# A gated delta rule on one core: from a pipeline of single steps to rounds of two steps

## The chip, the cores and the metric

One core of a Trainium2 chip runs the whole program. The metric is the device time of one execution in microseconds, as the median of several runs. Engines are called as in the profile: PE is TensorE's matmul, PEld its weight load, DVE is VectorE, ACT is ScalarE, POOL is GpSimd, SP is SyncE, which here only issues DMAs.

## The reference, cut to what matters

A backbone of two layers over 512 latent tokens and 256 context tokens of width 1024, in float32. Layer 0 is a bidirectional gated delta rule, layer 1 is attention. The change lies in layer 0's recurrence over chunks of 64 tokens, run for 16 value heads in both directions. Head size is 128 for keys and values. The state s is 128 x 128 per head and direction.

```python
def step(s, xs):
    qk_i, qd_i, kd_i, u_i, w_i, gl_i = xs
    v_new = u_i - jnp.einsum('bhcd,bhde->bhce', w_i, s)
    o = jnp.einsum('bhcd,bhde->bhce', qd_i, s) + jnp.einsum('bhcs,bhse->bhce', qk_i, v_new)
    s = s * gl_i[..., None, None] + jnp.einsum('bhcd,bhce->bhde', kd_i, v_new)
    return s, o
```

u and w are the inverse of a triangular matrix T, made per chunk beforehand, times scaled values and keys. The kernel uses T r with r = v - (decay) k s in place of u - w s, which is the same v_new, and applies the decays as scale factors of single tokens.

## The kernel before, in words

**Tiles.** Both directions run at once: one half of the 128 partitions holds a chunk of the forward pass, the other half a chunk of the backward pass. There are 12 chunk steps s (4 over the context, 8 over the latents). Each is cut into four parts p of four value heads (two key heads). So the loop has 48 steps x = 4 s + p. Each token tile (two chunks of 64) is met twice, since each direction reaches it from its own end; `visit` says which time it is.

**One step x.** `products(x)` (line 1490) makes, for each of the two key heads j, a PSUM tile `ks` with four products of 128x64 shape: k s and q s for both directions (line 1508). DVE turns the k s half into `r` (line 1511), ACT scales the q s half into the output tile `O` or, at the second visit, into `o` (line 1514), and POOL decays the state `S` (line 1517). At the second visit POOL also adds `o` to `O` (line 1520). `solve(x)` (line 1523) makes T r with 64x64 tiles in `pr` (line 1534), ACT copies it to `vn` (line 1536) and makes four decayed copies `vd` (line 1546; by DVE, line 1544, for s = 0). `update(x)` (line 1549) makes Q K v_new in `pq` (line 1560) and the state update in `su` (line 1568), both with 64x64 tiles. DVE then adds `pq` to `O` (line 1574) and `su` to the state (line 1582, two instructions; a copy, line 1580, for s = 0). Step 11 updates no state. Each of the matmuls that the code names runs as two instructions.

**Order.** The loop at line 1687 issues products(x), solve(x - 1), update(x - 2), so three steps are in flight. Inside `manual_schedule` (line 1678) PE, DVE, ACT and POOL take the instructions in the order of the program; the loads on SP aren't in that order and go out as their buffers come free. `load_step` (line 1462) asks for a chunk step's k, q, v, T, QK and the turned keys kt. All but q have one buffer for even and one for odd steps.

**PSUM.** The pool `psC` holds two buffers of `ks`, one of `pr`, one of `pq` and one of `su`. `pr` and `pq` are allocated with room for four heads' pairs, of which half is written. A buffer is given to a new tile when everything that read the old one is done.

**Around it.** Between the steps the loop issues `square_o` (ACT, sums of squares of finished outputs), a chain of small steps on DVE and POOL for the norm's factors, and the beginning of the output projection: `out_load`, `gate_load` (DMA), `out_high` (ACT, the weights' upper half), `out_low` (POOL, the lower half), `out_scale` (ACT), `out_turn` (PE, transposes into a `ks` buffer), `out_gated`, `out_rest` (DVE), `out_product` (PE, in the buffers of `pr`, `pq`, `su`).

Of the kernel before, what the change touches and what calls it, by code (L numbers as in the profile page):

```python
# [75 lines left out]
def raw(ap, offset, dims):  # L76
    return bass.AP(ap.tensor, ap.offset + offset, [list(ap.ap[0])] + [list(d) for d in dims])


def bcast(ap, axis, n):  # L80
    a = ap.unsqueeze(axis)
    shape = list(a.shape)
    shape[axis] = n
    return a.to_broadcast(shape)


def backbone(tc, a, out):
# [1335 lines left out]
    def square_o(t, h):  # L1423
        S.activation(ojk[:, h % 2], O[t][:, h], AF.Square, accum_out=oss[:, SLOT[t], h:h + 1])
# [21 lines left out]
    if True:  # L1446
# [38 lines left out]

        live = {}

        def products(x):  # L1490

            s, p = divmod(x, 4)
            if p == 0:
                load_step(s)
            t, visit = where(s)
            kq, kt, v, Tt, QK = loads[s]
            if s == 0:
                live[x] = [v[:, 4 * p:4 * p + 4]]
                return
            r = ch.tile([P, 4, P], F32, tag="r", name=f"r{x}", bufs=2)  # L1500
            o = O[t][:, 4 * p:4 * p + 4] if visit == 0 else ch.tile([P, 4, P], F32, tag="o", name=f"o{x}", bufs=2)
            for j in range(2):
                hh = 2 * p + j
                ks = pcx.tile([P, 2, 2, P], F32, tag="ks", name=f"ks{x}_{j}", bufs=2)
                for w in range(2):
                    for d in range(2):
                        r0 = (visit ^ d) * 64
                        T.matmul(ks[r0:r0 + 64, w], kq[w][:, hh, r0:r0 + 64], St[hh][:, d], start=True, stop=True)  # L1508
                for i in range(2):
                    h = 2 * hh + i  # L1510
                    V.scalar_tensor_tensor(r[:, 2 * j + i], ks[:, 0, i], negV[:, visit, t, h:h + 1], v[:, h], ALU.mult, ALU.add)
                for i in range(2):
                    h = 2 * hh + i
                    S.activation(o[:, 2 * j + i], ks[:, 1, i], AF.Copy, scale=egV[:, visit, t, h:h + 1])
                if s < 11:
                    g_ = glb[:, visit, :, t, 2 * hh:2 * hh + 2]
                    G.tensor_tensor(St[hh], St[hh], bcast(g_, 3, P), ALU.mult)  # L1517
            if visit == 1:
                oh = O[t][:, 4 * p:4 * p + 4]
                G.tensor_tensor(oh, oh, o, ALU.add)  # L1520
            live[x] = [r]

        def solve(x):

            s, p = divmod(x, 4)
            t, visit = where(s)
            Tt = loads[s][3]
            r, = live[x]
            pr_ = pcx.tile([P, 2, 4, P], F32, tag="pr", name=f"pr{x}", bufs=1)
            for i in range(2):  # L1530
                for j in range(2):
                    for hf in range(2):
                        r0, o0 = hf * 64, (hf ^ j) * 64
                        T.matmul(pr_[o0:o0 + 64, j, i], Tt[r0:r0 + 64, 4 * p + 2 * j + i, :], r[r0:r0 + 64, 2 * j + i], start=True, stop=True)
            vn = ch.tile([P, 4, P], F32, tag="vn", name=f"vn{x}", bufs=2)
            S.copy(vn.rearrange("p (j i) d -> p j i d", j=2), pr_[:, :, 0:2])
            vd = None
            if s < 11:
                vd = ch.tile([P, 4, P], F32, tag="vd", name=f"vd{x}", bufs=2)
                for c in range(4):  # L1540
                    h = 4 * p + c
                    el = (elX if c > 1 else elV)[:, visit, t, h:h + 1]
                    if s == 0:
                        V.tensor_scalar(vd[:, c], vn[:, c], el, None, ALU.mult)
                    else:
                        S.activation(vd[:, c], vn[:, c], AF.Copy, scale=el)
            live[x] = [vn, vd]

        def update(x):

            s, p = divmod(x, 4)
            t, visit = where(s)
            kq, kt, v, Tt, QK = loads[s]
            vn, vd = live.pop(x)
            po = pcx.tile([P, 2, 4, P], F32, tag="pq", name=f"pq{x}", bufs=1)
            for i in range(2):
                for j in range(2):
                    for hf in range(2):
                        r0, i0 = hf * 64, (hf ^ j) * 64
                        T.matmul(po[r0:r0 + 64, j, i], QK[i0:i0 + 64, 4 * p + 2 * j + i, :], vn[i0:i0 + 64, 2 * j + i], start=True, stop=True)  # L1560
            if s < 11:
                su = pcx.tile([P, 2, 2, 2, P], F32, tag="su", name=f"su{x}", bufs=1)
                for j in range(2):
                    hh = 2 * p + j
                    for c0 in (0, 64):
                        for d in range(2):
                            r0 = (visit ^ d ^ j) * 64
                            T.matmul(su[c0:c0 + 64, d ^ j, j], kt[r0:r0 + 64, hh, c0:c0 + 64], vd[r0:r0 + 64, 2 * j:2 * j + 2], start=True, stop=True)  # L1568
            oh = O[t][:, 4 * p:4 * p + 4]
            ov = oh.rearrange("p (j i) d -> p j i d", j=2)  # L1570
            if s == 0:
                S.copy(ov, po[:, :, 0:2])
            else:
                V.tensor_tensor(ov, po[:, :, 0:2], ov, ALU.add)
            if s < 11:
                for j in range(2):
                    hh = 2 * p + j
                    sj = raw(su[:, 0, 0] if j == 0 else su[:, 1, 1], 0, [[512 - 1024 * j, 2], [P, 2], [1, P]])
                    if s == 0:
                        V.tensor_copy(St[hh], sj)  # L1580
                    else:
                        V.tensor_tensor(St[hh], sj, St[hh], ALU.add)  # L1582

    PASS = ((0, 0), (0, 1), (1, 0))
    SCALE = 128.0 ** -0.5
# [93 lines left out]
    def some(steps, n):  # L1681
        for f_ in steps[:n]:
            f_()
        del steps[:n]

    squares = [(t, h) for t in (1, 0, 5) for h in range(VH)]
    for x in range(50):
        if x == 47:
            out_scale(0)
        if x < 48:  # L1690
            products(x)
        if 0 <= x - 1 < 48:
# [775 lines left out]
```

## Time and profile before

| what | us |
|---|---|
| median of 3 runs | 1166.88 |
| lowest and highest run | 1165.75, 1167.48 |
| span of the profiled execution (the profile gives no other time of it) | 1170.6 |
| PE busy | 1131.2 (97%) |
| PEld busy | 925.0 (79%) |
| DVE busy | 801.6 (68%) |
| ACT busy | 730.6 (62%) |
| POOL busy | 568.8 (49%) |
| first and last state product (line 1508) start | 560.7 and 728.8 |

Times in the profile count from the start of the span. A row of the timeline gives start, duration, engine, line, operation, what it writes and reads, and how many alike were merged; in brackets stands how long the engine was idle before it and what released it. A row of the busy times gives a stretch, its length, each engine's busy time with the number of instructions, the clock granted to PE (1.00 is full), the share of the DMA engines' time and GB/s. A matmul's end is modelled, and the next one is issued before it.

### The profile page before, as it was taken

The page shows a single profiled execution, that of the slowest core. Times are in us where ns is not written, and L with a number is a line of the kernel's source. Part 1 is how long each engine was busy: PE and PEld are TensorE (multiplying, and loading weights), DVE is VectorE, ACT ScalarE, POOL GpSimd, SP SyncE. Part 2 cuts the span into 40 slices and gives each one's busy share as a digit, 9 for nine tenths or more (in the row PEclk, how much of TensorE's full clock was granted, in tenths as well). Part 3 has the DMA queues.
Part 4 walks back from the last instruction along what each step waited for, and adds up shares of the span by engine and source line. Part 5 has one row for each costly group of instructions (what it writes and reads, how often), then busy time and mean ns, then how long its engine had stood idle before and what let it go on. Part 6 is the DMA issues. An engine that isn't in the chain of part 4 may idle for free. (4 is left out here: it accounts for less than half of the span.)

```text
span 1170.6 us, 27671 instructions
## 1 busy us (share of the span) xinstructions
PE 1131.2 (97%) x10767; PEld 925.0 (79%) x10767; DVE 801.6 (68%) x1657; ACT 730.6 (62%) x1908; POOL 568.8 (49%) x471
## 2 busy tenths in 40 slices
PE   5999999999999999989999999999999999999996
PEld 3677888888888888878666666788887889999885
DVE  5595565688897889673778888345557476667646
ACT  5434444477877889654678998775753246666731
POOL 0154000149989999910475587655745143130810
PEclk9999999999999999989999999999999999999998
DMA  9677754675748767445999994575844112101313
GB/s 366 240 272 223 279 154 140 210 184 174 215 124 258 246 219 261 162 160 190 243 260 246 276 257 113 198 214 183 247 135 135 36 55 73 37 19 55 109 72 90
DMA packets 118901, 208.73 MB, mean 178 GB/s; under 512 B 12497, under 2 KB 77170, under 8 KB 114930
## 3 DMA queue, kind: packets, MB, share of 16 engines
q1 hardware_dynamic: 98834, 195.32, 54.1%
q10 hardware_dynamic: 19936, 11.64, 3.4%
q8 instruction: 85, 1.39, 0.5%
q14 instruction: 46, 0.38, 0.1%
HBM read 166.16 MB, written 40.67 MB: 177 GB/s over the span
## 5 line engine op out<-in xcount | busy, mean ns | idle before, releaser
L1517 POOL TENSOR_TENSOR S<-S,glb 128x512 f32<-128x512 f32 x80 | 81.8, 1044 | 103.9 <-PE ks L1508 103.9
L1675 PE MATMUL po<-woh,y 128*128 128x512 f32 x384 | 130.0, 403 | 0.7 <-ACT y L1651 0.7
L1624 POOL TENSOR_TENSOR wol<-wo,woh 128x1024 fp32r<-128x1024 f32 x32 | 77.2, 2414 | 55.7 <-ACT woh L1617 51.9
L791 POOL TENSOR_TENSOR X<-X,tmp 128x62 f32<-128x62 f32 (+15 forms) x93 | 99.7, 1072 | 7.3
L790 POOL TENSOR_TENSOR tmp<-L,X 128x62 f32<-128x62 f32 (+15 forms) x93 | 92.8, 998 | 6.8
L904 PE MATMUL g_v<-uh,wh_v 128*128 128x512 f32 (+1 forms) x256 | 88.6, 346 | 2.7 <-DVE sil_v L938 2.7
L904 PE MATMUL g_z<-uh,wh_z 128*128 128x512 f32 (+1 forms) x256 | 89.0, 348 | 0.0
L919 DVE SCALAR_TENSOR_TENSOR acc_v<-g_v,cwv,acc_v 128x510 f32<-128x510 f32 (+3 forms) x128 | 78.3, 614 | 13.8 <-ACT acc_v L911 10.2
L904 PE MATMUL g_v<-uh,wl_v 128*128 128x512 f32 (+1 forms) x256 | 86.9, 339 | 0.0
L904 PE MATMUL g_v<-ul,wh_v 128*128 128x512 f32 (+1 forms) x256 | 86.8, 339 | 0.0
L904 PE MATMUL g_z<-uh,wl_z 128*128 128x512 f32 (+1 forms) x256 | 86.8, 339 | 0.0
L904 PE MATMUL g_z<-ul,wh_z 128*128 128x512 f32 (+1 forms) x256 | 86.7, 339 | 0.0
L1675 PEld LDWEIGHTS po<-woh,y 128*128 128x128 f32 x384 | 72.7, 189 | 16.0 <-ACT y L1651 0.9
L1675 PE MATMUL po<-wol,y 128*128 128x512 f32 x192 | 76.0, 396 | 0.9 <-POOL wol L1624 0.9
L1649 DVE SCALAR_TENSOR_TENSOR pt<-pt,og,z 128x128 f32<-128x128 f32 x96 | 34.4, 358 | 34.1 <-PE pt L1640 31.8
L1582 DVE TENSOR_TENSOR S<-su,S 128x512 f32<-128x512 f32 x80 | 51.6, 686 | 6.1 <-PE su L1568 3.9
L904 PEld LDWEIGHTS g_v<-uh,wh_v 128*128 128x128 f32 x256 | 49.0, 191 | 8.3 <-DVE sil_v L938 2.9
L464 POOL TENSOR_TENSOR wl_k<-w_k,wh_k 128x1024 fp32r<-128x1024 f32 x8 | 19.1, 2393 | 74.3 <-ACT wh_k L460 74.3
L1508 PE MATMUL ks<-S,ck 128*64 128x256 f32 x352 | 55.2, 392 | 0.0
L492 DVE SCALAR_TENSOR_TENSOR acc_k<-g_k,cwv,acc_k 128x510 f32<-128x510 f32 (+3 forms) x64 | 39.2, 615 | 23.3 <-ACT acc_k L485 21.6
L893 POOL TENSOR_TENSOR wl_z<-w_z,wh_z 128x1024 fp32r<-128x1024 f32 x3 | 7.3, 2445 | 97.6 <-ACT wh_z L890 97.6
L904 PEld LDWEIGHTS g_z<-uh,wh_z 128*128 128x128 f32 x256 | 48.9, 191 | 5.6 <-DVE sil_v L938 0.2
(448 smaller groups left out, 3384.8 us busy)
## 6 DMA issues: line engine op xcount, KB each, us to landing
aw<-in_ada_late SPq DMA_DIRECT2D x16, 1024.0 KB, 7.6
wo<-in_dn_w_out SPq DMA_DIRECT2D x32, 512.0 KB, 3.7
cv<-v_d SPq DMA_DIRECT2D x48, 256.0 KB, 8.0
aw<-in_ada_first SPq DMA_DIRECT2D x8, 1024.0 KB, 11.9
w_z<-in_dn_w_in SPq DMA_DIRECT2D x16, 512.0 KB, 4.8
w_v<-in_dn_w_in SPq DMA_DIRECT2D x16, 512.0 KB, 4.5
v_d<-vt ACTq DMA_DIRECT2D x16, 384.0 KB, 4.6
cT<-t_d SPq DMA_DIRECT2D x12, 512.0 KB, 8.1
```

Source lines behind the costliest of these rows:

```text
L464: E.tensor_tensor(khl[h][1][:, :, :m], kw.pop(h)[:, :, :m], khl[h][0][:, :, :m], ALU.subtract)
L492: V.scalar_tensor_tensor(acc[:, c0 + lo:c0 + hi], ps[:, lo + j - 2:hi + j - 2], cwv[:, j, 8 + h:9 + h], acc[:, c0 + lo:c0 + hi], ALU.mult, ...
L790: G.tensor_tensor(tv, bcast(L[:, :, j + 1:, j], 3, j + 1), bcast(X[:, :, j, 0:j + 1], 2, n), ALU.mult)
L791: G.tensor_tensor(X[:, :, j + 1:, 0:j + 1], X[:, :, j + 1:, 0:j + 1], tv, ALU.subtract)
L904: T.matmul(ps[:, :m], w[:, k], u[:, k, c0:c0 + m], start=k == 0 and n_ == 0, stop=k == KT - 1 and n_ == 2)
L919: V.scalar_tensor_tensor(acc[:, c0 + lo:c0 + hi], ps[:, lo + j - 2:hi + j - 2], cwv[:, j, ct:ct + 1], acc[:, c0 + lo:c0 + hi], ALU.mult, A ...
L1508: T.matmul(ks[r0:r0 + 64, w], kq[w][:, hh, r0:r0 + 64], St[hh][:, d], start=True, stop=True)
L1517: G.tensor_tensor(St[hh], St[hh], bcast(g_, 3, P), ALU.mult)
L1582: V.tensor_tensor(St[hh], sj, St[hh], ALU.add)
L1624: G.tensor_tensor(wl, raws.pop(n), halves[n][0], ALU.subtract)
L1649: V.scalar_tensor_tensor(pj, pj, og, raw(z, off, [[st_, 2], [1, 64]]), ALU.mult, ALU.mult)
L1675: T.matmul(acc[:, nh], y[i][:, j, :], ww[k][:, nh * 512:(nh + 1) * 512], start=h == 0 and x == 0, stop=h == VH - 1 and x == 2)
```

## The change

The single steps become 23 rounds of two steps x and y = x + 1, and a tail for steps 46 and 47 written out by hand. In a round PE gets the state products of both steps first (four `ks` tiles, still two buffers), then the 64x64 products: the state update of the round before's first step, Q K v_new of both steps of the round before, T r of x, the state update of the round before's second step, T r of y. The `pr` tile holds T r of both steps, and `pq` Q K v_new of both. Their copies to `vn` come at the end of the round, the decayed copies `vd` among the next round's state products, and the additions of `pq` to `O` one round later still, among the state products. Squares, the norm's chain and the output projection's first pieces are distributed anew. In the cut diff "..." marks what is left out; `states(x, j)` has the body of the old loop over j, and `solve`, `intra`, `update` have the old matmuls.

```diff
--- before
+++ after
-        def products(x):
...
-            for j in range(2):
-                hh = 2 * p + j
-                ks = pcx.tile([P, 2, 2, P], F32, tag="ks", name=f"ks{x}_{j}", bufs=2)
-                for w in range(2):
-                    for d in range(2):
-                        r0 = (visit ^ d) * 64
-                        T.matmul(ks[r0:r0 + 64, w], kq[w][:, hh, r0:r0 + 64], St[hh][:, d], start=True, stop=True)
-                for i in range(2):
-                    h = 2 * hh + i
-                    V.scalar_tensor_tensor(r[:, 2 * j + i], ks[:, 0, i], negV[:, visit, t, h:h + 1], v[:, h], ALU.mult, ALU.add)
-                for i in range(2):
-                    h = 2 * hh + i
-                    S.activation(o[:, 2 * j + i], ks[:, 1, i], AF.Copy, scale=egV[:, visit, t, h:h + 1])
-                if s < 11:
-                    g_ = glb[:, visit, :, t, 2 * hh:2 * hh + 2]
-                    G.tensor_tensor(St[hh], St[hh], bcast(g_, 3, P), ALU.mult)
-            if visit == 1:
-                oh = O[t][:, 4 * p:4 * p + 4]
-                G.tensor_tensor(oh, oh, o, ALU.add)
             live[x] = [r]
...
+        def begin(x):
...
+            live["o", x] = o
+
+        def states(x, j):
...
+            hh = 2 * p + j
+            ks = pcx.tile([P, 2, 2, P], F32, tag="ks", name=f"ks{x}_{j}", bufs=2)
...
+        def joined(x):
...
+            if s and visit == 1:
+                oh = O[t][:, 4 * p:4 * p + 4]
+                G.tensor_tensor(oh, oh, live["o", x], ALU.add)
+
+        def paired(x, tag):
+
+            if x % 2 == 0:
+                shared[tag] = pcx.tile([P, 2, 4, P], F32, tag=tag, name=f"{tag}{x}", bufs=1)
+            i0 = x % 2 * 2
+            return shared[tag][:, :, i0:i0 + 2]
...
-            pr_ = pcx.tile([P, 2, 4, P], F32, tag="pr", name=f"pr{x}", bufs=1)
+            pr_ = paired(x, "pr")
...
-            S.copy(vn.rearrange("p (j i) d -> p j i d", j=2), pr_[:, :, 0:2])
...
+            live[x] = [vn, pr_]
+
+        def kept_new(x):
+
+            vn, pr_ = live[x]
+            S.copy(vn.rearrange("p (j i) d -> p j i d", j=2), pr_)
+            vd = ch.tile([P, 4, P], F32, tag="vd", name=f"vd{x}", bufs=2) if x < 44 else None
+        def decayed_new(x, cs):
...
+            vn, vd = live[x]
+            for c in cs:
+                h = 4 * p + c
+                el = (elX if c > 1 else elV)[:, visit, t, h:h + 1]
+                if s == 0:
+                    V.tensor_scalar(vd[:, c], vn[:, c], el, None, ALU.mult)
+                else:
+                    S.activation(vd[:, c], vn[:, c], AF.Copy, scale=el)
-        def update(x):
...
-            po = pcx.tile([P, 2, 4, P], F32, tag="pq", name=f"pq{x}", bufs=1)
+        def intra(x):
...
+            po = paired(x, "pq")
...
+        def added(x):
...
+            ov = O[t][:, 4 * p:4 * p + 4].rearrange("p (j i) d -> p j i d", j=2)
             if s == 0:
-                S.copy(ov, po[:, :, 0:2])
+                S.copy(ov, po)
             else:
-                V.tensor_tensor(ov, po[:, :, 0:2], ov, ALU.add)
+                V.tensor_tensor(ov, po, ov, ALU.add)
+        def update(x):
...
@@ -1684,40 +1725,84 @@
-    for x in range(50):
-        if x == 47:
-            out_scale(0)
-        if x < 48:
-            products(x)
-        if 0 <= x - 1 < 48:
-            solve(x - 1)
-        if x == 48:
-            pt = out_gated(0)
-        if x == 49:
-            out_product(0, 2)
-        if 0 <= x - 2 < 48:
-            update(x - 2)
-        if 18 <= x < 34 or x >= 35:
-            for t, h in squares[:2]:
-                square_o(t, h)
-            del squares[:2]
-        if x == 1:
+
+    def squared(n):
+        for t, h in squares[:n]:
+            square_o(t, h)
+        del squares[:n]
+
+    for rd in range(23):
+        x, y = 2 * rd, 2 * rd + 1
+        first, second = x - 2, x - 1
+        begin(x)
+        begin(y)
+        decayed_new(first, (0,))
+        states(x, 0)
+        decayed_new(first, (1,))
+        if x >= 4:
+            added(x - 4)
+        states(x, 1)
+        decayed_new(first, (2, 3))
+        joined(x)
+        states(y, 0)
+        decayed_new(second, (0,))
+        if x >= 4:
+            added(x - 3)
+        states(y, 1)
+        decayed_new(second, (1, 2, 3))
+        joined(y)
+        if rd:
+            update(first)
+            intra(first)
+            intra(second)
+        solve(x)
+        if rd:
+            update(second)
+        solve(y)
+        squared(4 if 9 <= rd < 17 or rd == 18 else 6 if rd in (19, 20) else 0)
+        if rd == 22:
+            out_high(0)
+            out_low(0)
+        kept_new(x)
+        kept_new(y)
+        if rd == 0:
             V.tensor_tensor(or2, rq, rq, ALU.mult)
-        if x in (43, 44, 45, 46):
-            some(chain, (4, 6, 6, 99)[x - 43])
+        if rd in (20, 21, 22):
+            some(chain, (0, 10, 99)[rd - 20])
         if x in (28, 32, 36, 40):
             with tc.issue_after(mark[0]):
                 (out_load if x < 36 else gate_load)((x - 28) // 4 % 2)
-        if x in (45, 46):
-            out_high(x - 45)
-        if x in (47, 48):
-            out_low(x - 47)
-        if x == 47:
-            out_load(2)
-            out_turn(0)
-        if x == 48:
-            out_rest(0, pt)
-            out_scale(1)
+    begin(46)
+    begin(47)
+    out_high(1)
+    out_low(1)
+    states(46, 0)
+    added(42)
+    out_scale(0)
+    states(46, 1)
+    added(43)
+    joined(46)
+    states(47, 0)
+    states(47, 1)
+    joined(47)
+    intra(44)
+    intra(45)
+    out_turn(0)
+    solve(46)
+    kept_new(46)
+    solve(47)
+    kept_new(47)
+    added(44)
+    added(45)
+    out_load(2)
+    pt = out_gated(0)
+    out_rest(0, pt)
+    intra(46)
+    out_scale(1)
+    intra(47)
+    out_product(0, 2)
+    added(46)
+    added(47)
     out_turn(1)
```

More of the change, by code (lines that the diff above doesn't have):

```diff
@@ L1484, in load_step @@
             loads[s] = (kq, kt, v, Tt, QK)
-        live = {}
-        def products(x):
+        live, shared = {}, {}
+        def begin(x):
             s, p = divmod(x, 4)
@@ L1495, in products @@
             t, visit = where(s)
-            kq, kt, v, Tt, QK = loads[s]
+            v = loads[s][2]
             if s == 0:
@@ L1518, in products @@
-            if visit == 1:
-                oh = O[t][:, 4 * p:4 * p + 4]
-                G.tensor_tensor(oh, oh, o, ALU.add)
-            live[x] = [r]
+            live[x] = [r]
+            live["o", x] = o
+        def states(x, j):
+            s, p = divmod(x, 4)
+            if s == 0:
+                return
+            t, visit = where(s)
+            kq, _, v, _, _ = loads[s]
+            (r,), o = live[x], live["o", x]
+            hh = 2 * p + j
+            ks = pcx.tile([P, 2, 2, P], F32, tag="ks", name=f"ks{x}_{j}", bufs=2)
+            for w in range(2):
+                for d in range(2):
+                    r0 = (visit ^ d) * 64
+                    T.matmul(ks[r0:r0 + 64, w], kq[w][:, hh, r0:r0 + 64], St[hh][:, d], start=True, stop=True)
+            for i in range(2):
+                h = 2 * hh + i
+                V.scalar_tensor_tensor(r[:, 2 * j + i], ks[:, 0, i], negV[:, visit, t, h:h + 1], v[:, h], ALU.mult, ALU.add)
+            for i in range(2):
+                h = 2 * hh + i
+                S.activation(o[:, 2 * j + i], ks[:, 1, i], AF.Copy, scale=egV[:, visit, t, h:h + 1])
+            if s < 11:
+                g_ = glb[:, visit, :, t, 2 * hh:2 * hh + 2]
+                G.tensor_tensor(St[hh], St[hh], bcast(g_, 3, P), ALU.mult)
@@ L1523, in solve @@
+        def joined(x):
+            s, p = divmod(x, 4)
+            t, visit = where(s)
+            if s and visit == 1:
+                oh = O[t][:, 4 * p:4 * p + 4]
+                G.tensor_tensor(oh, oh, live["o", x], ALU.add)
[4 more added lines that the diff above has]
+            return shared[tag][:, :, i0:i0 + 2]
         def solve(x):
             s, p = divmod(x, 4)
-            t, visit = where(s)
@@ L1535, in solve @@
             vn = ch.tile([P, 4, P], F32, tag="vn", name=f"vn{x}", bufs=2)
[L1536 to L1546, printed above, removed]
+            live[x] = [vn, pr_]
[3 more added lines that the diff above has]
+            vd = ch.tile([P, 4, P], F32, tag="vd", name=f"vd{x}", bufs=2) if x < 44 else None
             live[x] = [vn, vd]
-        def update(x):
+        def decayed_new(x, cs):
+            if not 0 <= x < 44:
+                return
             s, p = divmod(x, 4)
             t, visit = where(s)
-            kq, kt, v, Tt, QK = loads[s]
-            vn, vd = live.pop(x)
-            po = pcx.tile([P, 2, 4, P], F32, tag="pq", name=f"pq{x}", bufs=1)
+            vn, vd = live[x]
+            for c in cs:
+                h = 4 * p + c
+                el = (elX if c > 1 else elV)[:, visit, t, h:h + 1]
+                if s == 0:
+                    V.tensor_scalar(vd[:, c], vn[:, c], el, None, ALU.mult)
+                else:
+                    S.activation(vd[:, c], vn[:, c], AF.Copy, scale=el)
+        def intra(x):
+            s, p = divmod(x, 4)
+            QK = loads[s][4]
+            vn, _ = live[x]
+            po = paired(x, "pq")
             for i in range(2):
@@ L1560, in update @@
                         T.matmul(po[r0:r0 + 64, j, i], QK[i0:i0 + 64, 4 * p + 2 * j + i, :], vn[i0:i0 + 64, 2 * j + i], start=True, stop=True)
[L1561 to L1568, printed above, removed]
@@ L1569, in update @@
-            oh = O[t][:, 4 * p:4 * p + 4]
-            ov = oh.rearrange("p (j i) d -> p j i d", j=2)
+            live["po", x] = po
+        def added(x):
+            s, p = divmod(x, 4)
+            t, _ = where(s)
+            po = live.pop(("po", x))
+            ov = O[t][:, 4 * p:4 * p + 4].rearrange("p (j i) d -> p j i d", j=2)
             if s == 0:
-                S.copy(ov, po[:, :, 0:2])
+                S.copy(ov, po)
             else:
-                V.tensor_tensor(ov, po[:, :, 0:2], ov, ALU.add)
@@ L1575, in update @@
[L1575 to L1582, printed above, removed]
+                V.tensor_tensor(ov, po, ov, ALU.add)
+        def update(x):
+            s, p = divmod(x, 4)
+            if s == 11:
+                return
+            t, visit = where(s)
+            kt = loads[s][1]
+            _, vd = live[x]
+            su = pcx.tile([P, 2, 2, 2, P], F32, tag="su", name=f"su{x}", bufs=1)
+            for j in range(2):
+                hh = 2 * p + j
+                for c0 in (0, 64):
+                    for d in range(2):
+                        r0 = (visit ^ d ^ j) * 64
+                        T.matmul(su[c0:c0 + 64, d ^ j, j], kt[r0:r0 + 64, hh, c0:c0 + 64], vd[r0:r0 + 64, 2 * j:2 * j + 2], start=True, stop=True)
+            for j in range(2):
+                hh = 2 * p + j
+                sj = raw(su[:, 0, 0] if j == 0 else su[:, 1, 1], 0, [[512 - 1024 * j, 2], [P, 2], [1, P]])
+                if s == 0:
+                    V.tensor_copy(St[hh], sj)
+                else:
+                    V.tensor_tensor(St[hh], sj, St[hh], ALU.add)
```

## The prediction

> **What bounds the kernel now.** I read the page first, then the busy time by stretch, then the timeline of one step, then the waits at both ends of the stage.
>
> ```profile
> span 1170.6 us, 27671 instructions
> ```
> ```profile
> core 0: us, PE busy (x) PEld busy (x) DVE busy (x) ACT busy (x) POOL busy (x), PEclk, DMA share, GB/s
> 560.70:624.00 63.30, 60.55 (x980) 39.66 (x976) 47.24 (x110) 45.13 (x137) 41.37 (x39) 1.00 1.06 251
> 624.00:724.30 100.30, 100.30 (x1718) 65.00 (x1714) 82.36 (x191) 92.41 (x332) 69.26 (x70) 1.00 0.91 241
> 724.30:738.50 14.20, 11.75 (x160) 7.70 (x157) 8.16 (x21) 8.07 (x22) 9.65 (x11) 0.88 0.23 57
> ```
> ```profile
> 640.00:660.00 20.00, 20.00 (x352) 12.94 (x344) 15.97 (x37) 18.82 (x69) 10.91 (x11) 1.00 1.03 279
> ...
> 680.00:700.00 20.00, 20.00 (x338) 12.83 (x338) 16.66 (x39) 18.28 (x68) 17.58 (x16) 1.00 0.98 263
> ...
> 730.00:735.00 5.00, 2.55 (x45) 1.58 (x38) 3.06 (x7) 3.38 (x11) 3.87 (x3) 0.97 0.15 43
> 735.00:740.00 5.00, 5.00 (x31) 3.53 (x32) 1.51 (x4) 1.05 (x1) 2.54 (x2) 0.69 0.72 197
> ```
>
> The delta rule's steps with a state product run from 560.70 to 738.5. From 624 on PE is never idle, so one step costs what PE takes for it. ACT (94% from 640 to 660) and DVE (80%) have little to spare.
>
> One step, by the timeline (start, duration, engine, line):
>
> ```profile
> 640.25 1.04 PE L1568 MATMUL su<-vd,ckt 64*64 64x256 f32 x16
> ...
> 641.23 0.65 PE L1508 MATMUL ks<-S,ck 128*64 128x256 f32 x4
> 641.29 0.69 ACT L1546 ACTIVATE vd<-vn,elV 128x128 f32<-128x128 f32 x2
> 641.45 1.29 DVE L1582 TENSOR_TENSOR S<-su,S 128x512 f32<-128x512 f32 x2 [0.19 <-PE su L1568]
> ...
> 641.71 0.60 PE L1508 MATMUL ks<-S,cq 128*64 128x256 f32 x4
> 641.89 0.68 ACT L1546 ACTIVATE vd<-vn,elX 128x128 f32<-128x128 f32 x2
> ...
> 642.14 0.60 PE L1508 MATMUL ks<-S,ck 128*64 128x256 f32 x4
> ...
> 642.40 2.05 POOL L1517 TENSOR_TENSOR S<-S,glb 128x512 f32<-128x512 f32 x2 [1.73 <-PE ks L1508]
> ...
> 642.57 0.60 PE L1508 MATMUL ks<-S,cq 128*64 128x256 f32 x4
> 642.66 1.17 DVE L1511 SCALAR_TENSOR_TENSOR r<-ks,negV,cv 128x128 f32<-128x128 f32 x4
> ...
> 643.11 0.67 PE L1534 MATMUL pr<-r,cT 64*64 64x128 f32 x16
> 643.36 1.20 ACT L1514 ACTIVATE O<-ks,egV 128x128 f32<-128x128 f32 x4 [0.20 <-DVE r L1511]
> ...
> 643.59 0.62 PE L1560 MATMUL pq<-vn,cQK 64*64 64x128 f32 x16
> ...
> 644.03 1.04 PE L1568 MATMUL su<-vd,ckt 64*64 64x256 f32 x16
> 644.35 0.69 DVE L1574 TENSOR_TENSOR O<-pq,O 128x512 f32<-128x512 f32 x1 [0.51 <-PE pq L1560]
> 644.44 0.59 ACT L1536 COPY vn<-pr 128x512 f32<-128x512 f32 x1
> ...
> 645.00 0.65 PE L1508 MATMUL ks<-S,ck 128*64 128x256 f32 x4
> ```
>
> The reader should see the period, 645.00 - 641.23 = 3.77 us, and its parts: four groups of state products (ks) 0.43 apart (the first 0.48), T r (pr) 0.48, Q K v (pq) 0.44, state updates (su) 0.97. The last ks group would let the next begin at 643.00; pr begins at 643.11. su needs 4 x 0.216 = 0.86 and takes 0.97. So each change between the 128x64 and the 64x64 shape costs 0.11 of PE, and the first group after it 0.05 more: 0.16 each, 0.32 a step.
>
> **The change part by part.** The edits that only regroup PE leave its matmuls as they are: two steps had four changes of shape and have two. Saved: 2 x 0.16 = 0.32 us a round. PE's own work in a round: 2 x 3.77 - 0.32 = 7.22. Rounds with state products before the tail: steps 4 to 45, so 21. Alone this is 21 x 0.32 = 6.7 us of gain.
>
> *The ks buffers.* Four ks tiles are now written one after another, and there are still two buffers; before, 1.9 us of 64x64 work stood between every two tiles and the next two. A buffer's trip, from its first matmul, by the rows: its second group starts at 0.48 and lasts 0.60, done at 1.08. The first reader follows by 0.09 (POOL at 642.40 after 642.31). Two r on DVE: four took 1.17 at 0.34 each, so 0.28 apart, together 0.62. ACT's scaling of the same tile starts only behind both (642.66 + 0.62 = 643.28, ACT 643.36 with "<-DVE r"): 0.08. Two scalings, likewise: 0.64. Then PE again, which needs the price of a released wait:
>
> ```profile
> 558.24 1.29 DVE L1580 COPY S<-su 128x512 f32<-128x512 f32 x2
> ...
> 559.68 1.09 PE L1568 MATMUL su<-vd,ckt 64*64 64x256 f32 x16 [0.74 <-DVE S L1580]
> ...
> 560.70 0.65 PE L1508 MATMUL ks<-S,ck 128*64 128x256 f32 x4
> ```
> ```profile
> 724.28 0.65 PE L1508 MATMUL ks<-S,ck 128*64 128x256 f32 x4
> ...
> 730.94 0.59 ACT L1536 COPY vn<-pr 128x512 f32<-128x512 f32 x1
> ...
> 731.59 0.67 PE L1534 MATMUL pr<-r,cT 64*64 64x128 f32 x16 [0.44 <-ACT vn L1536]
> ...
> 732.36 4.68 POOL L1624 TENSOR_TENSOR wol<-wo,woh 128x1024 fp32r<-128x1024 f32 x2
> ```
>
> PE follows ACT by 731.59 - 731.53 = 0.06 and DVE by 559.68 - 559.53 = 0.15. The trip is 1.08 + 0.09 + 0.62 + 0.08 + 0.64 + 0.06 = 2.57. PE is ready for the third tile at 0.48 + 3 x 0.43 = 1.77: **it waits 0.80**, in every round, with nothing else in its queue that could go ahead. Behind it stand all 64x64 products of the round.
>
> The fourth tile needs the second buffer. On DVE the old round's addition of po (0.69) now stands between the r of the first and of the second tile: r at 1.17, the addition at 1.72, the second r from 2.38 to 3.00, scalings from 3.08 to 3.72, PE at 3.78. Third tile done at 2.57 + 0.91 = 3.48: **another 0.30**. Bounds: 0 if that addition lay elsewhere, 0.8 if it is late as well; I take the sum of the rows.
>
> *The su buffer.* Two state updates of a round share one buffer. Before, S began 641.45 - 640.25 = 1.20 after su and both additions ended 2.49 after it, with 3.77 to the next su. Now only two pq and one pr stand between: 0.91 + 3 x 0.44 = 2.23. Second su at 2.49 + 0.06 to 0.15 behind the first: **a wait of 0.32 to 0.41**; I take 0.36.
>
> Sum of a round: -0.32 + 0.80 + 0.30 + 0.36 = +1.14, so 7.54 + 1.14 = 8.68 us, and 21 x 1.14 = **+23.9 us**.
>
> The trace shows here why throughput alone would mislead: per round ACT is busy 2 x 3.77 x 0.94 = 7.1, DVE 6.0, POOL at most 6.6 (680 to 700), all under PE's 7.22, which would give the 6.7 us of gain; the loss is in the trip of one buffer. A rule of the Trainium skill speaks the same way against packing the small products more densely (TensorEngine Tiling (Array Packing), PSUM Bottleneck: tiling speeds up the matmuls and not the emptying of PSUM, which may then be the limit). Read as throughput it would leave 7.22 a round here, read as the time until a buffer is free 8.68; the rows decide for the second.
>
> *The shared pr and pq tiles.* The copy of the first step's v_new is issued behind the second step's products into the same tile. I price it as waiting for them: they end 0.05 into the next round, two copies of 0.59 from 0.2 to 1.4, one decay 0.35, ACT free at 1.75; the first scaling is due at 1.08 + 0.09 + 0.62 + 0.08 = 1.87. Cost zero with 0.12 to spare; without that cover, each tenth late is a tenth on the round. The decays for the second su end about 7.0 and it starts at 7.4. po is added a round later, with pq free before the next pq.
>
> *Loads.* A step's loads are asked for at the same place in the program, SP is not in the written order, and each waits for its buffer. QK and kt come free later, by up to a round. A step loads v in four parts and k, q, kt, T and QK:
>
> ```profile
> cv<-v_d SPq DMA_DIRECT2D x42, 256.0 KB, 8.6
> cT<-t_d SPq DMA_DIRECT2D x11, 512.0 KB, 8.1
> ```
>
> That is 4 x 256 + 5 x 512 KB = 3.67 MB; at the 279 GB/s of 640 to 660 that is 13.2 us, in a step of 15.1 now and 17.4 then. Cost zero. A late load would show as PE waiting at pr or pq, as it may do now:
>
> ```profile
> 578.55 0.40 PE L1560 MATMUL pq<-vn,cQK 64*64 64x128 f32 x6
> ...
> 580.29 0.48 PE L1560 MATMUL pq<-vn,cQK 64*64 64x128 f32 x9 [1.34 <-issue]
> ```
>
> Such irregular holes, early on with the DMA share at 1.06, cost (724.28 - 560.70) - 42 x 3.77 = 5.2 us. With rounds 15% longer for the same bytes I count them as gone: -5.2; the other bound is 0.
>
> *Start and tail.* In the first two rounds the second v_new copy and one S copy come a little later for lack of interleaving: +0.4. In the tail the lower halves of the output weights (2.34 each on POOL, 732.36) are made earlier, which takes away PE waits of up to 2.45 (14.20 - 11.75). Against it stand the ks waits of 1.1, a wait of the last T r for the copy out of the shared tile (about 0.9), and the r of step 46 on DVE behind the norm's last factors, which wait for POOL. I take +0.7, between -2.4 and +3. The squares and casts are as many as before.
>
> Total: 23.9 - 5.2 + 0.4 + 0.7 = +19.8 on the profiled execution's 1170.6 of span. That span is 3.7 above the median of the three runs (1166.88), perhaps by those holes; the difference is carried over to the median: **1187 us**.
>
> **The rivals.**
>
> *Tile halves are free to go by themselves (faster).* If ACT's scaling needed only its own half of ks, and each S addition only its own half of su, the trip would be 2.57 - 0.70 = 1.87, the first wait 0.10, the others zero: 21 x (0.10 - 0.32) = -4.6, with start and tail -3.5, with the holes gone -8.7: 1158 to 1163, say **1161**. It turns at waits of 0.27 a round. Against it: ACT begins 0.08 behind the second r, and S 1.20 after su's start, though the first half's products are done after some 0.65 (two of its four groups).
>
> *Only the first wait shows.* The fourth tile and su are covered: 21 x (0.80 - 0.32) - 5.2 + 1.1 = +6: **1173**. For it: 0.30 and 0.36 are small beside the prices of a semaphore. Against: both are floors of chains without slack.
>
> *ACT joins the path.* If the 0.12 is overrun by half a microsecond (six squares in rounds 19 and 20, or v_new later than I have it): 21 x 0.5 = +10.5: **1197**.
>
> *The clock falls.* The stretch 724.30 to 738.50 has 17% PE idle and a clock of 0.88, and 735 to 740 shows 0.69 behind a half-idle 730 to 735. The new rounds are 1.46 / 8.68 = 17% idle. At 0.88 a round's 7.22 grows by 0.98: +20, **1207**. Against it: 580.29's hole of 1.34 and the others left the clock at 1.00 (560.70 to 624). This is what the Trainium skill describes for cycling through PSUM buffers (TensorE: Matmul & The Clock Gate, A second HAM failure mode: psum-queue depth-cycling: short PE pauses between groups that make the clock swing); the holes before 624 do not bear it out.
>
> **How the numbers follow.** Forecast 0.65 (its own range 1180 to 1194), first wait only 0.13, ACT on the path 0.10, clock 0.05, halves free 0.05, about no change 0.02. The range 1174 to 1198 leaves out the clock, the faster case and part of 1173. About 0.2% (2.3 us) is what a measurement of this kernel can tell from no change: faster 0.05, same 0.03, slower 0.92.
>
> **What would show it.** After: ks starts in a round at 0, 0.9, 2.6, 3.8 and a round of 8.5 to 8.8; PE's waits at ks for ACT o or O of 15 to 25 us in total; at su for DVE S about 7; the weight-load gap of 0.39 in front of pr half as often; DMA share lower; clock 1.00. Wrong if the third ks tile follows at 1.77, or if ACT is busy without a gap through a round.

## The result and the profile after

The changed kernel takes 1196.09 us (median of 5 runs, 1193.97 to 1196.87) against 1166.57 (5 runs of the kernel before on the same chip): 1.0248 times as long, 95% interval 1.0229 to 1.0267. It is 29.5 us slower; the forecast was 1187, in a range of 1174 to 1198.

Busy times by stretch of the kernel after (length, PE, PEld, DVE, ACT, POOL, clock, DMA share, GB/s):

```profile
core 0: us, PE busy (x) PEld busy (x) DVE busy (x) ACT busy (x) POOL busy (x), PEclk, DMA share, GB/s
...
562.00:640.00 78.00, 69.76 (x1142) 44.91 (x1138) 53.31 (x127) 53.84 (x172) 46.56 (x44) 1.00 0.97 233
640.00:742.00 102.00, 91.37 (x1451) 58.63 (x1452) 70.84 (x169) 80.64 (x291) 62.95 (x63) 1.00 0.75 204
742.00:765.00 23.00, 16.30 (x244) 11.31 (x237) 13.94 (x29) 11.64 (x30) 11.89 (x12) 0.93 0.21 62
```

PE, which before was never idle from 624 on, is now idle for a tenth of the steady stage. ACT (79%) and DVE (69%) became idler too: no engine took PE's place as the bound. The clock stayed at 1.00 from 562 to 742.

One round of it, by the timeline:

```profile
666.31 0.65 PE L1518 MATMUL ks<-S,ck 128*64 128x256 f32 x4
...
667.23 0.60 PE L1518 MATMUL ks<-S,ck 128*64 128x256 f32 x4
...
667.44 0.61 DVE L1521 SCALAR_TENSOR_TENSOR r<-ks,negV,cv 128x128 f32<-128x128 f32 x2
...
667.97 0.68 DVE L1602 TENSOR_TENSOR O<-pq,O 128x512 f32<-128x512 f32 x1
668.15 0.63 ACT L1524 ACTIVATE O<-ks,egV 128x128 f32<-128x128 f32 x2 [0.32 <-DVE r L1521]
668.57 0.60 DVE L1521 SCALAR_TENSOR_TENSOR r<-ks,negV,cv 128x128 f32<-128x128 f32 x2
...
668.83 0.65 PE L1518 MATMUL ks<-S,ck 128*64 128x256 f32 x4 [0.57 <-ACT O L1524]
...
669.26 0.62 ACT L1524 ACTIVATE O<-ks,egV 128x128 f32<-128x128 f32 x2 [0.20 <-DVE r L1521]
...
669.94 0.65 PE L1518 MATMUL ks<-S,ck 128*64 128x256 f32 x4
...
670.95 1.09 PE L1618 MATMUL su<-vd,ckt 64*64 64x256 f32 x16
...
672.19 1.29 DVE L1625 TENSOR_TENSOR S<-su,S 128x512 f32<-128x512 f32 x2 [0.51 <-POOL S L1527]
...
673.63 1.09 PE L1618 MATMUL su<-vd,ckt 64*64 64x256 f32 x16 [0.27 <-ACT ojk L1424]
...
674.87 1.29 DVE L1625 TENSOR_TENSOR S<-su,S 128x512 f32<-128x512 f32 x2 [1.39 <-PE su L1618]
...
675.09 0.65 PE L1518 MATMUL ks<-S,ck 128*64 128x256 f32 x4
```

The four ks tiles start at 0, 0.92, 2.52 and 3.63 of the round. The third starts 0.05 behind the end of ACT's scalings of the first tile (668.15 + 0.63 = 668.78), and those start behind DVE's two r. The second su comes 2.68 behind the first, 0.15 after the end of the state additions (672.19 + 1.29 = 673.48); the profile names ACT there, which made an unrelated square. In the same way it names POOL in front of the first additions, but these start 1.24 behind their su (672.19 - 670.95), as the second ones do, which waited for PE (674.87 - 673.63); and in the control below they start at 670.27, 0.10 before POOL's decays end. The round is 8.78, and so is every round with state products from the third to the last but one. The first two are 9.15 and 8.96, the last before the tail is 9.27; no irregular hole is in this execution.

The waits of PE from 562 to 742 us (total, times, longest):

```profile
engine line waited for: us in total, times, longest us
PE ks L1518 <- ACT o L1524: 6.9, 11, 1.1
PE ks L1518 <- ACT O L1524: 5.9, 11, 0.6
PE su L1618 <- ACT ojk L1424: 3.0, 11, 0.3
PE su L1618 <- DVE S L1625: 2.0, 8, 0.3
```

These count only the time with no matmul in flight, so they are shorter than the delays: the third tile starts 0.75 after it could (2.52 - 1.77) and its row says 0.57. The fourth tile's delay of 0.2 has no row there.

The tail, steps 46 and 47:

```profile
745.80 0.65 PE L1518 MATMUL ks<-S,ck 128*64 128x256 f32 x4
...
749.30 2.34 POOL L1665 TENSOR_TENSOR wol<-wo,woh 128x1024 fp32r<-128x1024 f32 x1
749.38 2.39 DVE L1437 SCALAR_TENSOR_TENSOR fo<-fo,rq 128x32 f32<-128x32 f32 x2 [2.52 <-POOL fo L221]
751.70 0.60 DVE L1521 SCALAR_TENSOR_TENSOR r<-ks,negV,cv 128x128 f32<-128x128 f32 x2
...
753.09 1.12 PE L1518 MATMUL ks<-S,ck 128*64 128x256 f32 x4 [5.34 <-ACT o L1524]
...
763.01 0.49 PE L1681 MATMUL pt<-ident,so 128*128 128x128 f32 x3
```

DVE stands at the norm's last factors, 2.52 for POOL's chain and 2.39 in the factors themselves; step 46's r stands behind them, and PE's third ks tile starts at 7.29 of this round. Its first four products took 1.12 where others take 0.65: from 752 to 757 the granted clock was 0.66.

### The profile page after: what moved, and what is told of

It is laid out like the page before. It is cut to its first block, busy times and chain, and to the rows that moved or that the text cites. A ratio compares the mean times of both kernels' runs of the same rounds, so it can differ in the third digit from the quotient of the medians.

```text
span 1193.9 us, 27570 instructions
## 1 busy us (share of the span) xinstructions
PE 1134.9 (95%) x10767; PEld 928.2 (78%) x10767; DVE 801.6 (67%) x1657; ACT 729.6 (61%) x1908; POOL 569.6 (48%) x471
## 4 chain that ended last, share of the span: by engine, by line
PE 84%; DVE 7%; ACT 5%; issue 2%; POOL 1%; DMA 1%; ACTq 0%; DVEq 0%; POOLq 0%
PE po L1716 11%; PE g_v L904 11%; PE g_z L904 11%; PE g_k L474 6%; PE g_q L904 6%; PE ks L1518 4%; PE pg L2144 3%; PE pg L2195 3%; PE po L2264 3%; PE kv L2029 3%; PE s L2215 3%; PE su L1618 2%; DVE r L1521 2%; PE pt L2243 2%; PE pa L300 2%
## 5 line engine op out<-in xcount | busy, mean ns | idle before, releaser
L1521 DVE SCALAR_TENSOR_TENSOR r<-ks,negV,cv 128x128 f32<-128x128 f32 x176 | 53.3, 345 | 20.7 <-PE ks L1518 19.3
L1618 PE MATMUL su<-vd,ckt 64*64 64x256 f32 x704 | 49.0, 393 | 7.2 <-ACT ojk L1424 3.0
L1518 PEld LDWEIGHTS ks<-S,ck 128*64 128x64 f32 x352 | 19.7, 137 | 45.5 <-ACT o L1524 23.1
L492 DVE SCALAR_TENSOR_TENSOR acc_k<-g_k,cwv,acc_k 128x510 f32<-128x510 f32 (+3 forms) x64 | 39.2, 615 | 23.3 <-ACT acc_k L485 21.6
```

## The experiments

Theory A on the changed kernel says that the trips of its PSUM buffers (ks, su) set the length of a round, and not what any engine has to do. A trip is the time from a buffer's first matmul to its next use. The rivals are PE's or ACT's amount of work, the sharing of pr and pq, and ACT's chain standing close behind.

**The kernel before once more.** No edit.

> The kernel before, unchanged, profiled once more. Theory A (the early holes at pr and pq belonged to the one profiled execution, whose span of 1170.6 is some 6 us over what the median leaves for a span): every step now comes 3.77 us after the last, steps 4 to 46 take 158.5 us, span near 1165. Theory B (they are a part of the kernel): holes of about 5 us again, span near 1170.

1169.87 us, span 1168.1: steps 13 and 15 came 6.78 and 5.66 us after the one before, the others nearly all 3.77, so 5.0 us of holes again, in other places than before. Theory A fell: the holes aren't of that one execution alone. A third trace of this loop, that of the last experiment below, has 4.1 us of them (162.6 for 158.5). But runs of this kernel in these comparisons reach from 1162.24 to 1174.53, and what the fastest of them do in that stage no trace here shows.

**Without Q K v, two ks buffers (control).** In `intra` the products go, and in `added` the additions:

```diff
-            po = paired(x, "pq")
...
+            if s == 0:
+                S.copy(O[where(s)[0]][:, 4 * p:4 * p + 4], live[x][0])
```

> The changed kernel without the Q K v products and their additions to O (O of the first step is a copy of v_new); that frees one PSUM pair, which is not used. It is the control for the next two. Theory A (a round is held by chains: ks buffer, su buffer): the fourth ks tile comes 0.2 earlier for lack of DVE's additions, second su stays 2.68 behind the first, round 8.78 to about 8.55, time about 1190. Theory B (PE's throughput): 0.87 less PE work in each of 21 rounds, 18 us, time about 1177.

One steady round:

```profile
664.63 0.65 PE L1518 MATMUL ks<-S,ck 128*64 128x256 f32 x4
...
667.15 0.65 PE L1518 MATMUL ks<-S,ck 128*64 128x256 f32 x4 [0.57 <-ACT O L1524]
...
668.07 0.60 PE L1518 MATMUL ks<-S,ck 128*64 128x256 f32 x4
...
669.03 1.09 PE L1604 MATMUL su<-vd,ckt 64*64 64x256 f32 x16
...
671.70 1.09 PE L1604 MATMUL su<-vd,ckt 64*64 64x256 f32 x16 [1.14 <-ACT ojk L1424]
...
673.16 0.65 PE L1518 MATMUL ks<-S,ck 128*64 128x256 f32 x4
```

Third tile at 2.52, fourth at 3.44 (without DVE's addition it needs no second wait), second su 2.67 behind the first: the round is 8.53 for the 8.55 expected, though PE has 0.87 less to do. Theory B falls. The time misled: 1204.65 us (1.0315, 1.0279 to 1.035), since the edit did more than it was to do. Nothing read QK any more, its buffers came free at once, its loads went ahead of k's and q's on SP, and PE waited for those:

```profile
PE ks L1518 <- DMA ck<-k_d: 4.9, 1, 4.9
...
PE ks L1518 <- DMA cq<-q_d: 2.2, 1, 2.2
```

Behind the first of these waits the granted clock was 0.50 (599.46 to 608.80). The steady rounds behind that stretch stay a fair control.

**Four ks tiles in two pairs, a first try.** The second step's two tiles were cut out of one allocation of the free pair, one half each.

```diff
+            if x % 2:
+                if j == 0:
+                    shared["more"] = pcx.tile([P, 2, 4, P], F32, tag="pq", name=f"kt{x}", bufs=1)
+                ks = shared["more"][:, j].rearrange("p (w i) d -> p w i d", w=2)
```

> As the control, and the second step's two ks tiles lie in the PSUM pair that is free now, so four ks tiles have four buffers. Theory A1 (the ks buffers alone cost about 1.0 a round): third and fourth tile at 1.78 and 2.64, first su at 3.6, round 7.75, 17 us under the control, about 1173. Theory A2 (behind the ks buffers ACT's chain stands nearly as late: two copies of v_new, four decays and four scalings, from 0.2 to 4.1): the tiles come at 1.78 and 2.64, but the first su waits for ACT's decays until about 4.1, round 8.25, 6 us under the control, about 1184. Theory C (buffers don't matter): as the control.

> As the kernel with four ks buffers, and ACT makes all four decays of a step ahead of the round's scalings (the second step's behind the scalings). Theory A2: the decays are ready at 2.6, the first su starts at 3.6, round 7.75, 17 us under the control, about 1173. Theory A1: no change against four buffers alone.

1218.08 (1.0426, 1.0347 to 1.0504) and 1214.89 us (1.0402, 1.0368 to 1.0436), slower than with two buffers. The first of the two:

```profile
663.62 0.60 PE L1523 MATMUL kt<-S,ck 128*64 128x256 f32 x4
...
666.31 0.65 PE L1523 MATMUL kt<-S,ck 128*64 128x256 f32 x4 [1.66 <-ACT O L1529]
```

The third tile came at once, at 1.78, but the fourth 2.69 behind it, after everything that read the third: two halves of one allocation wait for each other like one buffer in this program. No theory is decided by this.

**Four ks tiles, each a tile of its own.** A few elements of QK are read on POOL, so that its loads stay where they were. In the tail, the output projection's sums that lay in the freed pair use these tiles too.

```diff
+            ks = pcx.tile([P, 2, 2, P], F32, tag="kt" if x % 2 else "ks", name=f"ks{x}_{j}", bufs=2)
+            q_ = loads[s][4][:, 4 * p, 0:8]
+            G.tensor_tensor(held, q_, q_, ALU.add)
```

> The changed kernel without the Q K v products and their additions to O (a few elements of QK are still read on POOL at that place, so that its buffer comes free as before), and the PSUM pair freed by that holds the second step's two ks tiles, each a tile of its own: four tiles, four buffers. To be held against the steady rounds of the control with two buffers (8.53; third and fourth tile at 2.51 and 3.43, first su at 4.40). Theory A1 (the ks buffers alone hold the round): tiles at 1.78 and 2.64, first su at 3.6, second 2.67 behind it, round 7.73. Theory A2 (ACT's decays stand close behind: in the control they end at 3.91 of the round): the first su starts at 3.97, round 8.10. Theory C (buffers don't matter): 8.53.

> The kernel with four ks tiles in four buffers, and ACT makes the four decays of the first step ahead of the round's scalings, those of the second behind them. Theory A2: the decays are ready at 2.4, the first su starts at 3.6, round 7.73. Theory A1: no change against the four buffers alone.

1176.24 us (1.0076, 1.0042 to 1.0109) and 1172.28 us (1.0037, 1.0014 to 1.0059). A steady round of the first:

```profile
630.80 0.65 PE L1519 MATMUL ks<-S,ck 128*64 128x256 f32 x4
...
632.58 0.60 PE L1519 MATMUL ks<-S,ck 128*64 128x256 f32 x4
...
633.44 0.60 PE L1519 MATMUL ks<-S,ck 128*64 128x256 f32 x4
...
634.02 0.69 ACT L1579 ACTIVATE vd<-vn,elX 128x128 f32<-128x128 f32 x2
634.41 1.09 PE L1607 MATMUL su<-vd,ckt 64*64 64x256 f32 x16
...
637.08 1.09 PE L1607 MATMUL su<-vd,ckt 64*64 64x256 f32 x16 [1.14 <-ACT vd L1579]
...
638.54 0.65 PE L1519 MATMUL ks<-S,ck 128*64 128x256 f32 x4
```

Tiles at 1.78 and 2.64, first su at 3.61, round 7.74 in both kernels: theory A1 to a hundredth. With the ks buffers alone the round falls from 8.53 to 7.74. A2 fell: su starts at 634.41 while ACT works on the second half of `vd` until 634.71, and its first half reads only the first half of `vd`. The 2.67 between the two su is unchanged; with a wait of 1.14 it is the next bound.

**ACT reads something else.** The scalings take v, not the q half of ks.

```diff
-                S.activation(o[:, 2 * j + i], ks[:, 1, i], AF.Copy, scale=egV[:, visit, t, h:h + 1])
+                S.activation(o[:, 2 * j + i], v[:, h], AF.Copy, scale=egV[:, visit, t, h:h + 1])
```

> The changed kernel, but ACT's scalings read v in SBUF in place of the q half of the ks tile (so the outputs lack Q S; the products are made all the same). A ks buffer is then free when DVE's two r are made. Theory A (a buffer's trip is the sum of its readers one behind the other): trip 2.52 less ACT's share of about 0.65, third tile at 1.9, fourth at 3.0 (DVE's addition of po stands between the r), first su at 4.0 for 4.64, round 8.14 for 8.78, 13 us less, about 1183. Theory B (ACT's own amount of work holds the round): its scalings are as many and as long, 8.78, 1196.

1184.13 us (1.0144, 1.0111 to 1.0176). A steady round:

```profile
617.65 0.65 PE L1518 MATMUL ks<-S,ck 128*64 128x256 f32 x4
...
619.54 0.65 PE L1518 MATMUL ks<-S,ck 128*64 128x256 f32 x4
...
620.65 0.65 PE L1518 MATMUL ks<-S,ck 128*64 128x256 f32 x4
...
621.67 1.09 PE L1618 MATMUL su<-vd,ckt 64*64 64x256 f32 x16
...
625.80 0.65 PE L1518 MATMUL ks<-S,ck 128*64 128x256 f32 x4
```

The third tile of a round starts at 1.89, the fourth at 3.00, the first su at 4.02, and the round is 8.15. ACT has no less to do (two scalings take 0.69 for 0.63), but the buffer's trip is shorter by its share. Theory B falls.

**The second su later.** T r of the second step ahead of it.

```diff
+        solve(y)
         if rd:
             update(second)
-        solve(y)
```

> The changed kernel, and T r of a round's second step is issued ahead of the second state update, not behind it, so that 0.44 more of PE's work lies between the two su. Theory A: PE's wait in front of the second su (0.45 by the profile) falls to about zero; the state additions end later and push the next round's r by about 0.3, so a round of 8.65 for 8.78, time about 1193. Theory A3 (the whole wait is a gain): 8.34, 1187. Theory B (su's wait is not what holds the round): 8.78.

```profile
611.40 0.65 PE L1518 MATMUL ks<-S,ck 128*64 128x256 f32 x4
...
614.19 0.65 PE L1518 MATMUL ks<-S,ck 128*64 128x256 f32 x4 [0.85 <-ACT O L1524]
...
619.00 1.09 PE L1618 MATMUL su<-vd,ckt 64*64 64x256 f32 x16
...
620.02 0.65 PE L1518 MATMUL ks<-S,ck 128*64 128x256 f32 x4
```

The round is 8.62 for the 8.65 expected, PE no longer waits at the second su, and the third tile comes at 2.79 for 2.52: most of the gain is given back one step on. The time, 1196.00 us (1.0262, 1.022 to 1.0304), shows none of it; this execution had holes in five rounds (8.96, 9.11, 8.75, 9.85 and a first one of 9.71).

**One part alone.** The kernel before, with only the state products of two steps together and, for that, a third buffer of `r`; pr and pq not shared.

```diff
-        if x < 48:
-            products(x)
+        if x < 48 and x % 2 == 0:
+            products(x)
+            products(x + 1)
```

> The kernel before with one part of the change: the state products of steps x and x + 1 are issued together, ahead of the two steps' 64x64 products; pr and pq are not shared, copies, decays and additions stay where they were, r has three buffers, the tail is as before. Theory A (the grouping is the loss, with two buffers each way): third tile at about 2.5, fourth at 3.4, and the second su behind its decays, a round of about 9.1, time about 1200. Theory B (sharing pr and pq, with the copies held behind the second T r, is the loss): two steps in 7.2 to 7.5, 1160 to 1166.

1202.62 us (1.0314, 1.0276 to 1.0353); steady rounds of 9.10 to 9.26:

```profile
652.74 0.65 PE L1508 MATMUL ks<-S,ck 128*64 128x256 f32 x4 [0.85 <-ACT O L1514]
...
658.18 1.09 PE L1568 MATMUL su<-vd,ckt 64*64 64x256 f32 x16 [0.48 <-DVE S L1582]
```

These are the same two waits, without any shared tile. The third tile comes at 2.79 here and the fourth at 3.71, later than the expected 2.5 and 3.4. So the grouping is the loss. The whole change has rounds of 8.78, so its other parts save 0.3 to 0.5 of it; which of them do, no run separates.

**The norm's factors later.** In the tail they and ACT's first output scaling stand behind the last state products.

```diff
-    out_scale(0)
     states(46, 1)
...
+    some(chain, 99)
+    out_scale(0)
     intra(44)
```

> The changed kernel, and the norm's last two factors on DVE and the scaling of the first output unit on ACT come behind the last state products, not ahead of them. Theory A (in the tail DVE stands behind these factors, which wait for POOL, and PE behind DVE): in the last round the third and fourth ks tile start at about 2.9 and 4.1, not 7.29 and 9.05, 3 to 5 us less in the tail, some time lost again where the transposes wait for the factors: 1192 to 1194. Theory B (the tail is bound by the copies of v_new and the output weights): no change, 1196.

1187.92 us (1.0189, 1.0151 to 1.0227). Third and fourth tile of the last round start at 2.79 and 3.71 for 7.29 and 9.05; the tail up to the second unit's transposes is 12.8 for 17.2 us. So the change's loss of 4.4 us in the tail came from DVE's queue, but not by the wait alone: the granted clock in that stretch is 1.00 here and was 0.90, which is up to 1.7 of it (a tenth of 17.2). The median fell by more, 8.2. In the profiled executions the rest lies ahead of every edited line: the first state product starts at 555.62 here and at 560.42 there, 4.8 earlier with the same code in front of it. The mean clock of the whole run is 0.994 here and 0.988 there; what sets it, no run here shows. So the 8.2 is no price of the factors.

**The kernel before with its own tail mended.** Upper and lower halves of the output weights one step earlier.

```diff
-        if x in (45, 46):
-            out_high(x - 45)
-        if x in (47, 48):
-            out_low(x - 47)
+        if x in (44, 45):
+            out_high(x - 44)
+        if x in (46, 47):
+            out_low(x - 46)
```

> The kernel before, with the output weights' upper halves (ACT) and lower halves (POOL) of the first two units made one step earlier. In the profile before PE waits 1.2 us for the first lower half in the tail. Theory A: that wait goes, tail 13 for 14.2, time 1 to 1.5 us less, which the runs can hardly tell from no change. Theory B (PE waits for the first unit's y, the lower halves hide behind it): no change.

1167.34 us (1.0015, 0.9989 to 1.0041): no change. The wait for the lower half is gone, and another stands in its place, 2.44 us at the transposes for ACT. The tail wasn't shorter in this execution, 15.7 us for 13.9, at a clock of 0.75 for 0.88:

```profile
730.79 0.90 PE L1640 MATMUL pt<-ident,so 128*128 128x128 f32 x3 [2.44 <-ACT o L1514]
```

None of these kernels is faster than the one before.

## Why the prediction was right, and where it was off

The mechanism and its three places were as predicted. The number was less good: 1196.1 lies inside the range of 1174 to 1198, but near its upper end and above the forecast's own 1180 to 1194.

- *Saving of 0.32 a round.* The changes of shape fell to two a round; first su still follows the last ks group with 0.1 of a gap. With four buffers tiles run at 1.78 and 2.64, the places given by the rows of before.
- *First ks wait, 0.80:* measured 0.75 (2.52 - 1.77). Four buffers take it away; with ACT out of the trip 0.12 of it is left. PE's rows for ks and ACT add up to 18.2 from 555 to 765, 5.3 of it in the tail, for the 15 to 25 forecast.
- *Second, 0.30:* measured about 0.2 (3.63 - 2.52 - 0.91). Without DVE's addition it is gone, as the prediction put it.
- *su, 0.36:* measured 0.46. Between the two su lie 2.68 us, and PE's work there is 2.22. The additions began 1.24 behind su for the 1.20 of before, and PE followed DVE by the upper of the two prices, 0.15. The rest of the 1.24 that a round grew, for the 1.14 predicted, is some 0.05 for each restart of PE behind a wait, which the sum left out. Two of the waits came out smaller than predicted and one larger, so the closeness of 1.14 to 1.24 is in part luck.
- *Rounds:* 745.80 - 560.42 = 185.4 us for the 163.6 of before, +21.8; predicted were 23.9 - 5.2 = 18.7. The regular part, 8.78 against 7.55 in 21 rounds, is 25.8 by itself. The first two rounds and the last are together 1.0 longer than regular ones, where the sum had 0.4 for the start.
- *The tail, +0.7:* measured +3.3 (763.01 - 745.80 = 17.2 for 738.21 - 724.28 = 13.9, each to the second transposes; clock 0.90 and 0.88). The prediction named the chain (r of step 46 behind the norm's factors) and gave it no number of its own. The factors waited 2.52 and took 2.39, and the later ks tiles then paid the buffer's trip after it. With the factors moved the tail was 4.4 shorter, clock included.
- *The holes, -5.2, and the base:* this is where most of the 9 us were lost. Between the two profiled executions the term came out as predicted, with no holes after; their spans grew by 23.3 (1170.6 to 1193.9) for the 19.8 of the sum. The medians grew by 29.5. The difference was carried over to a median well below the profiled execution of before: that took about 1172.4 by an estimate (its span and the 1.8 by which times exceed spans in these runs), and the median is 1166.57. With zero for the term the same sum gives 1192. But that it is the holes that the median lacks isn't shown. All three traces of this loop have them (5.2, 5.0 and 4.1), in executions of about 1172.4, 1169.87 and 1172.43, none of them at the median. Other stretches vary too: the first state product starts at 560.70, 557.73 and 559.86 in them.

With the measured rounds and tail, and nothing for the holes, the sum is 1166.9 + 21 x 1.24 + 1.0 + 3.3 = 1197.2 for 1196.1. Its terms were put in after the result, so this only says that no large term is missing if the median has no holes.

The rivals. Halves of a tile that come free by themselves fell for ks (ACT starts behind both r) and for su's additions, but it is how su reads `vd`. "Only the first wait shows" fell: 0.2 and 0.46 are not small beside the prices of a semaphore, which are 0.05 to 0.15 in these rows. ACT did not join the path: in the rounds with squares the period is 8.78 as in the others, and ACT stands idle for 0.32 in front of a round's first scaling, so the shared `pr` cost nothing, as predicted. That its number, 1197, is the nearest to the measured one is chance. The clock did not fall in the steady stage: it was 1.00, with PE idle for a tenth. So what the Trainium skill describes for cycling through PSUM buffers (TensorE: Matmul & The Clock Gate, A second HAM failure mode: psum-queue depth-cycling) is not borne out here by pauses of 0.57 us. Low clocks stood behind longer waits, 0.50 behind the 4.9 of the control and 0.66 behind the 5.34 of the tail; how long a wait it takes isn't shown.

## What to carry to other kernels

Before work is grouped to save a cost per change, count the buffers between producer and readers, and add up one buffer's trip: fill, first reader, second reader, release. Here 0.32 us a round were saved and 1.56 paid (1.24 + 0.32), with every engine below full. What stood between two uses of a buffer was not overhead but the cover of its trip. An experiment that leaves work out should keep its buffers' readers, or the loads change their order. And a difference between two profiled executions is not one between medians: first see how far each of the two lies from its median.

## What the hardware showed unexpectedly

The two DVE instructions of the norm's factors in the tail (line 1437, 32 and 16 columns) took 2.31 and 0.16, though one of 48 columns takes 0.21 elsewhere. The first ended at 751.69, with POOL's long subtraction (749.30 + 2.34 = 751.64), beside which it had begun. Both instructions read two operands from SBUF. In the kernel before, the first took 1.01 and ended at 729.01, with an addition on POOL that ended at 728.96; with the factors later, the two took 0.61 and 1.29, again beside work on POOL. The Trainium skill says as much (SBUF — State Buffer, Who interferes with whom: a DVE instruction with two SBUF inputs contends with a GpSimd instruction that reads SBUF, and the pair of ports that they share is an exclusive lock); the rows agree. r, with one input from PSUM, kept its 0.6 for two beside POOL's decays of 2.05.

Two halves of one PSUM allocation behaved as one buffer here (2.69 us between the tiles), two allocations did not (0.86). Whether the chip asks for that or only the program's own waits, no run separates.
